# Which PSUM banks take the transposes of layer A's outputs and the samples' product, and at which priority v and the outputs are read

## The chip, the cores and the metric

The kernel runs on one core of a Trainium2 chip. The metric is the device time of one execution in microseconds. A core has five engines that run side by side and meet at semaphores: TensorE (PE, matmuls and transposes), VectorE (DVE), ScalarE (ACT), GpSimd (POOL) and SyncE (SP, which issues the transfers). PE writes its results to PSUM, eight banks, from where ACT and DVE read them. A bank can be given to the next tile only when everything that reads the tile before has ended.

## What is computed

A decoder trunk of two layers for a prompt of 1024 tokens and 8 samples of one token each, side by side as 1032 columns, in float32. Layer A is HGRN2, a gated linear recurrence; layer B is a gated MLP over chunks of 128 tokens. Each is followed by a gated input embedding. The change touches layer A alone. Its core, cut from the reference:

```python
proj = h @ w_in
q, f, i, z = jnp.split(proj, [D_MODEL, 2 * D_MODEL, 2 * D_MODEL + D_INNER], axis=-1)
q = jax.nn.silu(q)                     # 8 heads of 128
logf = jnp.logaddexp(jnp.log(lb), jnp.log1p(-lb) + jax.nn.log_sigmoid(f))
k = -jnp.expm1(logf)
v = i                                  # 8 heads of 256
# S_t = diag(f_t) S_(t-1) + k_t v_t^T,  o_t = S_t^T q_t
o, S = hgrn2_chunkwise(q, k, v, logf, s0)
o = rmsnorm(o, g_norm)                 # over the 256 values of a head
return (o * jax.nn.silu(z)) @ w_out, S
```

The prompt starts from a state of zero; each sample brings its own state, which is updated by one token and multiplied with its q.

## The kernel before

**Precision.** Matmuls work on fp32 numbers that are split in two parts: `split` (L224) has ACT write the rounded high part (L225, named with h: `vh`, `kh`, `Sh`) and DVE the remainder (L226, named with l). `mm3` (L228) makes one product of three matmuls, L230 to L232. Both halves of a split read the same source, so a PSUM bank that is split is held until DVE's L226 has run.

**Tiling.** The 1032 columns come in three chunks of 384, 384 and 264. For each of the eight heads `head_proj` (L695) runs the projections for f, q and v, each into a tile `ps_proj` of the tag mm. Of q, ACT makes a sigmoid (`sg`, L616) and DVE multiplies (L617). Of v, ACT copies to `vf` (L717), PE transposes in blocks of 128 to `pt_v` (L760) and `split` makes `vh` and `vl`, with the samples' eight rows copied to `vs` (L763). `decay` (L801) makes the products of the forget gates (L813 to L822 and L848, most of DVE's work) and, through `visit`, the within-chunk attention in two further banks (`pC`, `pD`). `recur` (L892) goes through the blocks of 128 rows: `pd`, the state's update, and `po`, the output. `out_sum` (L872) has ACT copy the output to `on` (L876) and sum its squares (L877); `out_scale` (L880) adds epsilon on DVE (`ss_e`, L883) and takes the power on POOL (`rsq`, L239); ACT scales `on` (L935); `out_transpose` (L886) turns it by PE to `pt_o` (L889), and DVE multiplies `pt_o` with the gate to `oz` (L942). `sample` (L952) does the same for the eight samples: the product with the states is `pos` (L984), and its `pt_o` is read by DVE at L997.

**The PSUM banks.** In layer A the eight banks are: three of tag mm, in turn for `ps_proj`, `pt_k` (the transposes of k, L862), `pt_o` of the sample, and, at the end, `ps_pple` of the next stage; one of tag po for `po` and `pos`; one of tag pt for `pt_v` and the `pt_o` of the prompt; two for `pC` and `pD`; one for `pd`. From the time at which the last head's projections begin (`last_head`), `pos` is in mm; that holds for the samples of head 6 and of head 7.

**What sets the order.** PE's order is that of the program: generators that are spawned on a clock (`Ticks`, L49) and resumed after so many ticks (`yield`). One tick passes with each projection. The orders of the other engines are made by a scheduler that estimates times and goes by priority; `tc.high_priority(offset=PRI)` with `PRI = 400` puts what it encloses ahead of 400 later instructions' worth of program. ACT, DVE and SP therefore change their order if the priority or the bank of one instruction changes, and every engine runs its own order strictly.

Of the kernel before, what the change touches and what calls it, by code (L numbers as in the profile page):

```python
# [8 lines left out]
F32 = mybir.dt.float32  # L9
# [8 lines left out]
P = 128  # L18
# [8 lines left out]
DV = 256  # L27
# [3 lines left out]
PRI = 400  # L31
# [13 lines left out]
NT = (3, 3, 2)  # L45
# [37 lines left out]
def trunk_kernel(ctx, tc, xT, st, pT, nrm, wina, lbl, gna, wouta, winb, lng, lnb, lngr, lnbr,  # L83
# [7 lines left out]
    def pool(stack, name, bufs=1, **kw):  # L91
        return stack.enter_context(tc.tile_pool(name=name, bufs=bufs, reuse_waits="tile", **kw))
# [5 lines left out]
    pp = pool(ctx, "psum", space=PSUM)  # L98
# [125 lines left out]
    def split(hi, lo, src, eng=V):  # L224
        last["split"] = A.copy(hi, src)  # L225
        last["lo"] = eng.tensor_tensor(lo, src, hi.bitcast(F32), ALU.subtract)  # L226
# [393 lines left out]
    def new_head():  # L620
        return dict(f=[], qk=[], vh=[], vl=[], zs={}, dec={}, oz={})
# [73 lines left out]
    def head_proj(h, r):  # L695
# [9 lines left out]
        else:  # L705
            for c in CH:
                tk.spawn(decay(h, r, c), 1 + 5 * c)
        r["vs"] = wa.tile([NS, DV], F32, name="vs", bufs=1)
        tk.spawn(sample(h, r), 1)
        tk.spawn(recur(h, r), 1)  # L710
        for m in range(2):
# [42 lines left out]
    def v_token_major(h, r, m, c, vf):  # L754
        if not m:
            r["vh"].append(wa.tile([P, NT[c], DV], F32R, name=f"vh{c}"))
            r["vl"].append(wa.tile([P, NT[c], DV], F32R, name=f"vl{c}"))
        pt = pp.tile([P, 3, P], F32, name="pt_v", tag="pt", bufs=1)
        for i in range(NT[c]):
            PE.transpose(pt[:, i, :], vf[:, i * P:(i + 1) * P], ident)  # L760
        if c == 2:
            PE.transpose(pt[:NS, 2, :], vf[:, 256:264], ident)
            V.tensor_copy(r["vs"][:, m * P:(m + 1) * P], pt[:NS, 2, :])  # L763
        split(r["vh"][c][:, :, m * P:(m + 1) * P], r["vl"][c][:, :, m * P:(m + 1) * P], pt[:, :NT[c], :])
        if m:
            r[f"v{c}"] = True
        return
        yield
# [101 lines left out]
    last_head = [False]  # L870

    def out_sum(po, ss):  # L872

        on = wa.tile([P, DV], F32, name="on", bufs=6)
        with tc.high_priority(offset=PRI if last_head[0] else 0):
            A.copy(on, po)  # L876
            A.activation(po, po, AF.Square, accum_out=ss)  # L877
        return on

    def out_scale(ss, n):  # L880
        e = wa.tile([P, n], F32, name=f"ss_e{n}", bufs=2)
        with tc.high_priority(offset=PRI):
            V.tensor_scalar(e, ss, DV * EPS, None, ALU.add)  # L883
        return rsqrt(wa, e, n)

    def out_transpose(on, tag="pt", bufs=1):  # L886
        pt = pp.tile([P, 2, P], F32, name="pt_o", tag=tag, bufs=bufs)
        for m in range(2):
            PE.transpose(pt[:, m, :], on[:, m * P:(m + 1) * P], ident)  # L889
        return pt  # L890

    def recur(h, r):  # L892

        S = Sh = Sl = None
        for c in CH:
            yield lambda: c in r["dec"] and r.get(f"v{c}")
            ah, al, qh, ql, kh, kl, t128 = r["dec"][c]
            ss = wa.tile([P, 3], F32, name="ss", bufs=2)
            ons = []
            for i in range(NT[c]):  # L900
                n = OFF[c] // P + i
                vh, vl = r["vh"][c][:, i, :], r["vl"][c][:, i, :]
                pd = pa.tile([P, DV], F32, name="pd", bufs=1)
                po = pp.tile([P, DV], F32, name="po", tag="po", bufs=1)
                mm3(pd, blk(kh, i), blk(kl, i), vh, vl, True, True)
                mm3(po, blk(ah, i), blk(al, i), vh, vl, True, n == 0)
                if n:
                    mm3(po, blk(qh, i), blk(ql, i), Sh, Sl, False, True)
                Sn = wa.tile([P, DV], F32, name="S", bufs=2)
                with tc.high_priority(offset=PRI):  # L910
                    if n == 0:
                        V.tensor_copy(Sn, pd)
                    else:
                        V.scalar_tensor_tensor(Sn, S, t128[:, i:i + 1], pd, ALU.mult, ALU.add)
                    S = Sn
                    if n < 7:
                        Sh = wa.tile([P, DV], F32R, name="Sh", bufs=2)
                        Sl = wa.tile([P, DV], F32R, name="Sl", bufs=2)
                        split(Sh, Sl, S)
                if n == 7:  # L920
                    nc.sync.dma_start(so_p[h], S)
                ons.append(out_sum(po, ss[:, i:i + 1]))
                yield 2
            tk.spawn(finish(h, r, c, ss, ons), 1)

    def finish(h, r, c, ss, ons):

        n = NT[c]
        if h < NH - 1:
            r["zs"][c] = wa.tile([P, 2, W[c]], F32, name=f"zs{c}")  # L930
            nc.sync.dma_start(r["zs"][c], zd[h][c])
            r[f"z{c}"] = True
        y = out_scale(ss[:, :n], n)
        for i in range(n):
            A.activation(ons[i], ons[i], AF.Copy, scale=y[:, i:i + 1])  # L935
        yield OD[0]
        yield lambda: r.get(f"z{c}")
        oz = r["oz"][c] = wa.tile([P, 2, 384], F32, name="oz", bufs=2)
        for i in range(n):
            pt = out_transpose(ons[i])  # L940
            with tc.high_priority(offset=PRI):
                V.tensor_tensor(oz[:, :, i * P:(i + 1) * P], pt, r["zs"][c][:, :, i * P:(i + 1) * P], ALU.mult)  # L942
            yield 1
        if c < 2:
            spill(h, r, c)
            spilled.add((h, c))

    def spill(h, r, c):
        w = W[c]
        nc.sync.dma_start(ozd[c][:, 2 * h:2 * h + 2, :], r["oz"][c][:, :, :w])  # L950

    def sample(h, r):  # L952

        q, f, k = r["qk"][2][:, 0, :], r["f"][2], r["qk"][2][:, 1, :]
        qs = wa.tile([P, 3, NS], F32, name="qs", bufs=1)
        G.tensor_copy(qs[:, 0, :], f[:, 256:264])
        G.tensor_copy(qs[:, 1, :], k[:, 256:264])
        qmv = qm.rearrange("p (c two) x -> p c (two x)", two=2)
        G.tensor_copy(qmv[:, :, 0:34:33], q[:, 256:264].rearrange("p (c two) -> p c two", two=2))
        Ss = []  # L960
        for j in range(2):
            S0 = wa.tile([P, 4, DV], F32, name="S0", bufs=2)

            nc.sync.dma_start(S0, st[h].rearrange("p (c two) v -> p two c v", two=2)[:, j])
            Ss.append(S0)
        yield lambda: r.get("v2")
        vd = dram.tile([NS, DV], F32, name=f"vd{h}")
        nc.sync.dma_start(vd, r["vs"])
        for j in range(2):
            S0 = Ss[j]  # L970
            vb = wa.tile([P, 4, DV], F32, name="vb", bufs=1)
            nc.sync.dma_start(vb, vd.rearrange("(c two) v -> two c v", two=2)[j].partition_broadcast(P))
            yield 2
            for c in range(4):
                b = 2 * c + j
                A.activation(S0[:, c, :], S0[:, c, :], AF.Copy, scale=qs[:, 0, b:b + 1])
                V.scalar_tensor_tensor(S0[:, c, :], vb[:, c, :], qs[:, 1, b:b + 1], S0[:, c, :],  # L977
                                       ALU.mult, ALU.add)
            nc.sync.dma_start(so_s[h].rearrange("p (c two) v -> p two c v", two=2)[:, j], S0)
        yield 4  # L980
        pos = pp.tile([P, DV], F32, name="pos", tag="mm" if last_head[0] else "po", bufs=3 if last_head[0] else 1)
        for j in range(2):
            for c in range(4):
                PE.matmul(pos[32 * c:32 * c + 32, :], qm[:, 2 * c + j, :], Ss[j][:, c, :],  # L984
                          start=j == 0, stop=j == 1)
        ss = wa.tile([P, 1], F32, name="ss1", bufs=1)
        on = out_sum(pos, ss)
        yield 1
        y = out_scale(ss, 1)
        A.activation(on, on, AF.Copy, scale=y)  # L990
        yield OD[1]
        yield lambda: r.get("z2") and 2 in r["oz"]
        pt = out_transpose(on, "mm", 3)
        oz = r["oz"][2]
        pv = pt.rearrange("p m (c x) -> p m c x", x=32)[:, :, :, 0:2]
        for m in range(2):
            V.tensor_tensor(oz[:, m, 256:264].rearrange("p (c x) -> p c x", x=2), pv[:, m],  # L997
                            r["zs"][2][:, m, 256:264].rearrange("p (c x) -> p c x", x=2), ALU.mult)
        yield 5
        spill(h, r, 2)  # L1000
# [12 lines left out]
    for h in range(NH):  # L1013
# [5 lines left out]
        r = new_head() if h else r0  # L1019
# [705 lines left out]
```

## Time and profile before

| | us |
|---|---|
| median of three runs | 1908.05 |
| lowest and highest | 1906.54, 1909.65 |
| the profiled execution | 1910.62 |
| its span in the trace | 1908.8 |

The page lists for each engine the time in which it was busy; PE's weight loads (PEld) run beside its matmuls. A row of the table of waits reads: engine, tile and line that waited, what it waited for last, microseconds in total, times, longest. A row of the windows gives a stretch of time, its length, the busy time of PE, PEld, DVE, ACT and POOL with the number of instructions, then the clock that was granted to PE (1.00 is full speed), the busy share of the transfer engines and GB/s. A row of the timeline gives start, duration, engine, line, operation, output and inputs, and in brackets the idle time of the engine ahead of it and what ended that.

The span in 40 slices, busy tenths of PE and of the clock:

PE 8999989899899898999999999999999999999997, clock 9 tenths or more throughout. One slice is 47.7 us; the second to the eighth head of layer A fill about the sixth to the sixteenth.

### The profile page before, as it was taken

What the parts mean: (1) busy time and instruction counts of PE and PEld (TensorE: products, weight loads), DVE (VectorE), ACT (ScalarE), POOL (GpSimd) and SP (SyncE); (2) the same over time, 40 slices, a digit from 0 to 9 for tenths busy, and PEclk for the clock granted to TensorE, in tenths of its full rate; (3) what the DMA queues carried; (4) which work ended last, traced back from release to release, by engine and by line L of the source; (5) the groups of instructions that cost most, each with busy time, mean ns of one, the idle gap of its engine ahead of it and who ended that gap; (6) DMA issues with size and microseconds to landing.
All of it is one profiled execution on the core that took longest, in us unless ns stands there. A gap on an engine that the chain in (4) does not pass through costs nothing.

```text
span 1908.8 us, 37135 instructions
## 1 busy us (share of the span) xinstructions
PE 1834.5 (96%) x14458; PEld 1795.6 (94%) x14458; DVE 1367.6 (72%) x2760; ACT 898.2 (47%) x1905; POOL 410.9 (22%) x407
## 2 busy tenths in 40 slices
PE   8999989899899898999999999999999999999997
PEld 7999988898889898999999999999999999999997
DVE  7765878678788677678583955567778878777655
ACT  6533455565465554625353644443333345434442
POOL 4000011111111110000042433344444542000222
PEclk9999999999999999999999999999999999999999
DMA  6233333335443335765233343323334546954223
GB/s 215 78 110 106 116 113 114 103 119 163 135 135 115 103 122 175 249 231 183 82 102 133 117 144 99 101 77 110 110 113 137 177 146 198 300 180 126 71 89 112
DMA packets 164560, 258.11 MB, mean 135 GB/s; under 512 B 16096, under 2 KB 136864, under 8 KB 163360
## 3 DMA queue, kind: packets, MB, share of 16 engines
q1 hardware_dynamic: 164384, 255.74, 42.3%
q8 instruction: 113, 1.85, 0.4%
q14 instruction: 63, 0.52, 0.1%
HBM read 182.88 MB, written 72.80 MB: 134 GB/s over the span
## 4 chain that ended last, share of the span: by engine, by line
PE 63%; DVE 18%; DMA 9%; ACT 4%; issue 3%; POOL 2%; SPq 1%; DVEq 0%; POOLq 0%; ACTq 0%
PE ps_proj L230 15%; PE ps_proj L231 15%; PE ps_proj L232 15%; PE ps_d L230 2%; PE ps_d L232 2%; PE ps_d L231 2%; DMA vb<-vd 2%; PE ps_o L230 2%; PE ps_o L232 2%; PE ps_o L231 2%; DVE wlo L152 1%; DVE S L977 1%; POOL rsq L239 1%; DVE qk L848 1%; DVE M L818 1%
## 5 line engine op out<-in xcount | busy, mean ns | idle before, releaser
L230 PE MATMUL ps_proj<-bh,whi 128*128 128x264 f32 (+1 forms) x2248 | 721.1, 321 | 1.4 <-ACT u L493 1.4
L231 PE MATMUL ps_proj<-bl,whi 128*128 128x264 f32 (+1 forms) x2248 | 705.1, 314 | 4.9 <-DVE bl L226 2.4
L232 PE MATMUL ps_proj<-bh,wlo 128*128 128x264 f32 (+1 forms) x2248 | 704.2, 313 | 1.0 <-DVE wlo L152 1.0
L231 PEld LDWEIGHTS ps_proj<-bl,whi 128*128 128x128 f32 x2248 | 427.4, 190 | 8.2 <-DVE bl L226 4.6
L230 PEld LDWEIGHTS ps_proj<-bh,whi 128*128 128x128 f32 x2248 | 427.1, 190 | 3.8 <-ACT u L493 1.9
L232 PEld LDWEIGHTS ps_proj<-bh,wlo 128*128 128x128 f32 x2248 | 426.1, 190 | 1.9 <-DVE wlo L152 1.9
L152 DVE TENSOR_TENSOR wlo<-wstg,whi 128x1024 fp32r<-128x1024 f32 x148 | 185.5, 1254 | 111.3 <-ACT whi L151 110.9
L151 ACT CAST whi<-wstg 128x1024 fp32r<-128x1024 f32 x148 | 155.2, 1049 | 141.8 <-PE ps_proj L231 120.9
L151 ACT CAST shi<-ssum 128x512 fp32r<-128x512 f32 x152 | 94.1, 622 | 189.6 <-PE ps_proj L231 88.7
L152 DVE TENSOR_TENSOR slo<-ssum,shi 128x512 fp32r<-128x512 f32 x152 | 114.2, 754 | 9.3 <-ACT shi L151 8.9
L239 POOL TENSOR_TENSOR rsq<-rms_e,mhalf 128x3 f32<-128x3 f32 x15 | 17.8, 1187 | 365.1 <-DVE rms_e L284 361.4
L230 PE MATMUL ps_proj<-xmh,shi 128*128 128x384 f32 x244 | 82.8, 340 | 0.3 <-DVE u L497 0.3
L232 PE MATMUL ps_proj<-xmh,slo 128*128 128x384 f32 x244 | 81.7, 335 | 0.0
L231 PE MATMUL ps_proj<-xml,shi 128*128 128x384 f32 x244 | 81.6, 335 | 0.0
L848 DVE TENSOR_TENSOR qk<-qk,t 128x384 f32<-128x384 f32 (+1 forms) x144 | 74.4, 520 | 7.9 <-PE pC L798 7.3
L230 PE MATMUL ps_o<-bh,whi 128*128 128x384 f32 (+1 forms) x232 | 73.2, 316 | 0.0
L232 PE MATMUL ps_o<-bh,wlo 128*128 128x384 f32 (+1 forms) x232 | 72.7, 313 | 0.0
L231 PE MATMUL ps_o<-bl,whi 128*128 128x384 f32 (+1 forms) x232 | 72.7, 313 | 0.0
L1516 POOL TENSOR_TENSOR s<-s,u 128x384 f32<-128x384 f32 (+1 forms) x48 | 54.6, 1138 | 69.4 <-DVE s L1510 68.8
L239 POOL TENSOR_TENSOR rsq<-ss_e,mhalf 128x3 f32<-128x3 f32 (+2 forms) x32 | 29.2, 912 | 172.5 <-DVE ss_e L883 160.4
L1255 DVE TENSOR_TENSOR tmp<-tmp,pj 128x384 f32<-128x384 f32 (+1 forms) x48 | 25.6, 533 | 55.9 <-ACT tmp L1254 52.2
L266 POOL TENSOR_TENSOR ssq<-ssq,tmp 128x384 f32<-128x384 f32 (+1 forms) x36 | 34.3, 953 | 108.0 <-ACT tmp L265 108.0
(376 smaller groups left out, 4146.5 us busy)
## 6 DMA issues: line engine op xcount, KB each, us to landing
wstg<-in_wina SPq DMA_DIRECT2D x48, 512.0 KB, 3.7
wstg<-in_winb SPq DMA_DIRECT2D x48, 512.0 KB, 4.0
pj<-ppd SPq DMA_DIRECT2D x16, 516.0 KB, 5.0
S<-in_st SPq DMA_DIRECT2D x16, 512.0 KB, 4.5
vb<-vd SPq DMA_DIRECT2D x16, 512.0 KB, 4.6
out_so_s<-S SPq DMA_DIRECT2D x16, 512.0 KB, 3.5
wstg<-in_wouta SPq DMA_DIRECT2D x16, 512.0 KB, 5.5
wstg<-in_wgate SPq DMA_DIRECT2D x16, 512.0 KB, 3.7
```

Of the source, the lines that this page charges most:

```text
L151: A.copy(hi, src)
L152: V.tensor_tensor(lo, src, hi.bitcast(F32), ALU.subtract)
L230: PE.matmul(ps, wh, xh, start=first, stop=False, skip_group_check=more)
L231: PE.matmul(ps, wh, xl, start=False, stop=False, skip_group_check=more)
L232: PE.matmul(ps, wl, xh, start=False, stop=last, skip_group_check=more)
L239: G.tensor_tensor(y, e, mhalf[:, :n], ALU.pow)
L266: eng.tensor_tensor(ssq, ssq, sq[:, :w], ALU.add)
L818: V.reciprocal(yv[:, :, 4:8], xv[:, :, 4:8])
L848: V.tensor_tensor(lev, lev, t2.rearrange("p two (n o) -> p two n o", o=1).broadcast_to([P, 2, n, lv]), ALU.mult)
L977: V.scalar_tensor_tensor(S0[:, c, :], vb[:, c, :], qs[:, 1, b:b + 1], S0[:, c, :], ALU.mult, ALU.add)
L1255: V.tensor_tensor(gt[:, :w], gt[:, :w], pj[:, OFF[c]:OFF[c] + w], ALU.mult)
L1516: G.tensor_tensor(s[:, :w], s[:, :w], us[mm, c][:, :w], ALU.mult)
```

## The change

1. `v_token_major`: the split of `pt_v` into `vh` and `vl` gets high priority.
2. `out_sum`: ACT's copy and square of an output always have high priority, not only in the last head.
3. `out_transpose`: every `pt_o` is in tag mm, three banks, not only the sample's; tag pt is left to `pt_v`.
4. `sample`: `pos` is always in tag mm; tag po is left to `po`.

```diff
--- before.py
+++ after.py
@@ -761,7 +761,8 @@
         if c == 2:
             PE.transpose(pt[:NS, 2, :], vf[:, 256:264], ident)
             V.tensor_copy(r["vs"][:, m * P:(m + 1) * P], pt[:NS, 2, :])
-        split(r["vh"][c][:, :, m * P:(m + 1) * P], r["vl"][c][:, :, m * P:(m + 1) * P], pt[:, :NT[c], :])
+        with tc.high_priority(offset=PRI):
+            split(r["vh"][c][:, :, m * P:(m + 1) * P], r["vl"][c][:, :, m * P:(m + 1) * P], pt[:, :NT[c], :])
         if m:
             r[f"v{c}"] = True
         return
@@ -872,7 +873,7 @@
     def out_sum(po, ss):
 
         on = wa.tile([P, DV], F32, name="on", bufs=6)
-        with tc.high_priority(offset=PRI if last_head[0] else 0):
+        with tc.high_priority(offset=PRI):
             A.copy(on, po)
             A.activation(po, po, AF.Square, accum_out=ss)
         return on
@@ -883,8 +884,8 @@
             V.tensor_scalar(e, ss, DV * EPS, None, ALU.add)
         return rsqrt(wa, e, n)
 
-    def out_transpose(on, tag="pt", bufs=1):
-        pt = pp.tile([P, 2, P], F32, name="pt_o", tag=tag, bufs=bufs)
+    def out_transpose(on):
+        pt = pp.tile([P, 2, P], F32, name="pt_o", tag="mm", bufs=3)
         for m in range(2):
             PE.transpose(pt[:, m, :], on[:, m * P:(m + 1) * P], ident)
         return pt
@@ -978,7 +979,7 @@
                                        ALU.mult, ALU.add)
             nc.sync.dma_start(so_s[h].rearrange("p (c two) v -> p two c v", two=2)[:, j], S0)
         yield 4
-        pos = pp.tile([P, DV], F32, name="pos", tag="mm" if last_head[0] else "po", bufs=3 if last_head[0] else 1)
+        pos = pp.tile([P, DV], F32, name="pos", tag="mm", bufs=3)
         for j in range(2):
             for c in range(4):
                 PE.matmul(pos[32 * c:32 * c + 32, :], qm[:, 2 * c + j, :], Ss[j][:, c, :],
@@ -990,7 +991,7 @@
         A.activation(on, on, AF.Copy, scale=y)
         yield OD[1]
         yield lambda: r.get("z2") and 2 in r["oz"]
-        pt = out_transpose(on, "mm", 3)
+        pt = out_transpose(on)
         oz = r["oz"][2]
         pv = pt.rearrange("p m (c x) -> p m c x", x=32)[:, :, :, 0:2]
         for m in range(2):
```

Lines behind L763 are one higher after the change. The instructions are the same on every engine; PE's and POOL's orders are the same row by row. What moves is ACT's, DVE's and SP's order, and which bank a tile is in.

**DVE, third head, where v's last block is split.** Names: `M` and `qk` with L813 to L823 and L848/L849 are the decays of the third chunk; `pC` and `al` the attention; `vl<-pt_v` the split; `oz<-pt_o` the outputs, and that of 8 columns (L997/L998) the sample's. Before:

```order
L226 TENSOR_TENSOR al<-pC,ah 128x384
L818 RECIPROCAL M<-M 128x32x4
L226 TENSOR_TENSOR vl_4541<-pt_v,vh_4540 128x2x128
L819 TENSOR_TENSOR M<-qk,M 128x256
L820 TENSOR_TENSOR M<-qk,M 128x256
L942 TENSOR_TENSOR oz<-pt_o,zs_4388 128x2x128
L848 TENSOR_TENSOR qk<-qk,t_4527 128x2x24x8
L822 TENSOR_TENSOR qk<-qk,f 128x256
L848 TENSOR_TENSOR qk<-qk,f 128x2x128
L848 TENSOR_TENSOR qk<-qk,t_4568 128x2x12x16
L848 TENSOR_TENSOR qk<-qk,t_4650 128x2x64x2
L997 TENSOR_TENSOR oz<-pt_o,zs_4388 128x8 x2
```

After:

```order
L818 RECIPROCAL M<-M 128x32x4
L226 TENSOR_TENSOR vl_4541<-pt_v,vh_4540 128x2x128
L943 TENSOR_TENSOR oz<-pt_o,zs_4388 128x2x128
L226 TENSOR_TENSOR al<-pC,ah 128x384
L819 RECIPROCAL M<-M 128x32x4
L849 TENSOR_TENSOR qk<-qk,t_4527 128x2x24x8
L820 TENSOR_TENSOR M<-qk,M 128x256
L821 TENSOR_TENSOR M<-qk,M 128x256
L849 TENSOR_TENSOR qk<-qk,t_4568 128x2x12x16
L998 TENSOR_TENSOR oz<-pt_o,zs_4388 128x8 x2
L226 TENSOR_TENSOR kl<-pt_k,kh 128x384
L943 TENSOR_TENSOR oz<-pt_o,zs_4388 128x2x128
```

The split and the first `oz` now stand ahead of the second reciprocal, the sample's read ahead of three qk products, and the third `oz` and `kl` come directly behind it.

**PE and DVE, second head, around the samples' product.** On PE, the same before and after but for the line numbers: the last projection matmul of q's second chunk, `pos`, one `pt_o`, and the first projection matmul of the third chunk.

```order
L232 MATMUL ps_proj<-bh_137,wlo 128x384
L984 MATMUL pos<-S_3251,qm 32x256 x4
L984 MATMUL pos<-S_3253,qm 32x256 x4
L889 MATMUL pt_o<-ident,on 128x128 x2
L230 MATMUL ps_proj<-bh_138,whi 128x264
```

In banks: before, `pos` is in po and `pt_o` in pt, and `ps_proj` takes the next mm bank. After, `pos` and `pt_o` take the next two mm banks, and `ps_proj` the third, which holds the projection of q that ended just ahead of `pos` until DVE has read it at L617. On DVE at that place, before:

```order
L883 TENSOR_SCALAR ss_e_4244<-ss 128x3
L848 TENSOR_TENSOR qk<-qk,f 128x2x192
L851 TENSOR_TENSOR t_4513<-t_4359 128x3
L848 TENSOR_TENSOR qk<-qk,t_4291 128x2x96x2
L848 TENSOR_TENSOR qk<-qk,t_4316 128x2x48x4
L617 TENSOR_TENSOR qk<-ps_proj,sg 128x384
L942 TENSOR_TENSOR oz<-pt_o,zs_4034 128x2x128
L819 TENSOR_TENSOR M<-qk,M 128x384
```

After:

```order
L884 TENSOR_SCALAR ss_e_4244<-ss 128x3
L849 TENSOR_TENSOR qk<-qk,f 128x2x192
L852 TENSOR_TENSOR t_4513<-t_4359 128x3
L849 TENSOR_TENSOR qk<-qk,t_4291 128x2x96x2
L849 TENSOR_TENSOR qk<-qk,t_4316 128x2x48x4
L617 TENSOR_TENSOR qk<-ps_proj,sg 128x384
L943 TENSOR_TENSOR oz<-pt_o,zs_4034 128x2x128
L820 TENSOR_TENSOR M<-qk,M 128x384
```

L617 keeps its neighbours: `ss_e`, three qk products, then L617, then `oz`.

**DVE, last head, where the loads for the next stage begin.** `bl_139<-zstg` is the split of gated outputs that were spilled and are loaded again, `wlo<-wstg` that of weights, `zs` the gate. Before:

```order
L383 TENSOR_TENSOR bl_139<-zstg,bh_136 128x768 x2
L647 SCALAR_TENSOR_TENSOR zs_9939<-ps_proj,gn_813,sg 128x384
L914 SCALAR_TENSOR_TENSOR S<-S,t_9736,pd 128x256
L226 TENSOR_TENSOR Sl<-S,Sh 128x256
L883 TENSOR_SCALAR ss_e_10264<-ss 128x3
L383 TENSOR_TENSOR bl_139<-zstg,bh_136 128x768 x2
L942 TENSOR_TENSOR oz<-pt_o,zs_9939 128x2x128
L152 TENSOR_TENSOR wlo<-wstg,whi 128x1024
```

After:

```order
L383 TENSOR_TENSOR bl_139<-zstg,bh_136 128x768 x2
L647 SCALAR_TENSOR_TENSOR zs_9939<-ps_proj,gn_813,sg 128x384
L915 SCALAR_TENSOR_TENSOR S<-S,t_9736,pd 128x256
L226 TENSOR_TENSOR Sl<-S,Sh 128x256
L884 TENSOR_SCALAR ss_e_10264<-ss 128x3
L383 TENSOR_TENSOR bl_139<-zstg,bh_136 128x768
L152 TENSOR_TENSOR wlo<-wstg,whi 128x1024
L943 TENSOR_TENSOR oz<-pt_o,zs_9939 128x2x128
```

`wlo` has passed the second `bl` and the `oz`. That `oz` reads the `pt_o` behind `pos`, and the `ps_proj` that follows on PE now takes that `pt_o`'s bank.

## The prediction

> **What bounds the kernel now.** I began with the page's busy times.
>
> ```profile
> span 1908.8 us, 37135 instructions
> PE 1834.5 (96%) x14458; PEld 1795.6 (94%) x14458; DVE 1367.6 (72%) x2760; ACT 898.2 (47%) x1905; POOL 410.9 (22%) x407
> ```
>
> TensorE (PE) is busy for 1834.5 of 1908.8 us, so only time in which PE stands still, or runs at a lower clock, can be won. Next come the windows: they say where PE stands still.
>
> ```profile
> 262.00:790.00 528.00, 482.00 (x4840) 460.73 (x4839) 397.60 (x977) 293.43 (x769) 65.60 (x89) 0.97 0.41 130
> 100.00:262.00 162.00, 160.09 (x1286) 158.05 (x1285) 117.85 (x239) 68.16 (x144) 6.99 (x16) 1.00 0.38 115
> ```
>
> The second to the eighth head of layer A and the last one's tail lie between 262 and 790 us: PE busy for 482.0 of 528 us (91%), mean granted clock 0.97. In the stretch ahead of them it is 99% and 1.00. So 46 of the 74 idle microseconds lie where the change acts, and VectorE (DVE) is busy for only 75% of that stretch: PE waits there for the order of DVE's work more than for its amount. The table of PE's waits names the places.
>
> ```profile
> PE pt_o L889 <- DVE vl L226: 20.8, 7, 4.7
> PE pt_v L760 <- DVE oz L942: 11.6, 15, 3.7
> PE po L230 <- ACT pos L877: 6.4, 5, 1.5
> PE pos L984 <- ACT po L877: 3.3, 3, 1.2
> ...
> PE pt_o L889 <- DVE oz L942: 2.9, 5, 1.2
> ...
> PE po L230 <- ACT po L877: 1.1, 1, 1.1
> ```
>
> These rows sum to 46.1 us, and all come from two PSUM banks: pt_o and pt_v share that of tag pt, pos and po that of tag po. The change aims at every one. Last comes the clock around one of the seven pt_o stalls.
>
> ```profile
> 361.40:364.80 3.40, 1.41 (x9) 1.09 (x7) 3.40 (x8) 1.14 (x3) 0.36 (x1) 1.00 0.39 155
> 364.80:368.20 3.40, 2.79 (x10) 2.82 (x11) 3.19 (x10) 0.51 (x1) 0.00 (x0) 0.50 0.02 5
> 272.63:279.46 6.83, 4.16 (x14) 4.16 (x15) 2.93 (x13) 2.73 (x8) 0.19 (x1) 0.50 0.00 0
> ```
>
> The column behind POOL is the granted clock. PE idles 1.99 us of the first stretch; the next 3.4 us run at 0.50. In the second head 6.83 us run at half. So a stall costs its length and then some matmuls at half speed, and a wait that goes gives both back.
>
> Here a rule of the Trainium skill can be weighed. "TensorE: Matmul & The Clock Gate", section "What's actually happening", has the clock halved after at least one idle window of about 3.4 us. This trace disagrees: 1.99 us idle in a stretch of 3.40 us was enough. By the rule stalls of 2 us would cost no clock; I go by the trace.
>
> **The change part by part.** PE's order is the same row by row, and nothing is added to or taken from any engine's work; only banks and the order on ACT, DVE and SP change. So every term is a wait of PE that goes or comes.
>
> *The pt_o stall (seven times).* The place in the third head, in time order, DVE and PE:
>
> ```profile
> 362.79 0.93 DVE L817 RECIPROCAL M<-M 128x128 f32<-128x128 f32 x1
> ...
> 363.65 0.48 DVE L226 TENSOR_TENSOR al<-pC,ah 128x384 fp32r<-128x384 f32 x1
> ...
> 364.06 0.93 DVE L818 RECIPROCAL M<-M 128x128 f32<-128x128 f32 x1
> ...
> 364.92 0.35 DVE L226 TENSOR_TENSOR vl<-pt_v,vh 128x256 fp32r<-128x256 f32 x1
> ...
> 365.41 0.66 PE L889 MATMUL pt_o<-ident,on 128*128 128x128 f32 x2 [2.60 <-DVE vl L226]
> ...
> 365.52 0.41 DVE L820 TENSOR_TENSOR M<-qk,M 128x256 f32<-128x256 f32 x1
> ...
> 366.11 0.42 DVE L942 TENSOR_TENSOR oz<-pt_o,zs 128x256 f32<-128x256 f32 x1 [0.18 <-PE pt_o L889]
> ...
> 366.45 0.55 DVE L848 TENSOR_TENSOR qk<-qk,t 128x384 f32<-128x384 f32 x1
> ...
> 366.51 0.52 PE L232 MATMUL ps_proj<-bh,wlo 128*128 128x384 f32 x1
> ...
> 366.83 0.52 PE L230 MATMUL ps_proj<-bh,whi 128*128 128x384 f32 x1
> ...
> 368.50 0.34 PE L230 MATMUL ps_proj<-bh,whi 128*128 128x384 f32 x1
> ...
> 368.68 0.34 PE L231 MATMUL ps_proj<-bl,whi 128*128 128x384 f32 x1
> ...
> 369.03 0.38 PE L889 MATMUL pt_o<-ident,on 128*128 128x128 f32 x2
> ...
> 369.45 0.24 DVE L997 TENSOR_TENSOR oz<-pt_o,zs 128x8 f32<-128x8 f32 x2 [0.85 <-PE pt_o L889]
> ...
> 369.58 0.38 PE L889 MATMUL pt_o<-ident,on 128*128 128x128 f32 x2
> ```
>
> PE is ready at 365.41 - 2.60 = 362.81. pt_o needs the bank that vl still reads, and vl stands behind two reciprocals. With its own bank pt_o runs at 362.8. The twelve matmuls behind it are then at full speed: starts 0.18 apart (368.50 to 368.68), not 0.32 (366.51 to 366.83), so 2.1 us from 363.1 to 365.2. Then come the sample's pt_o and pt_k, 0.55 as between 369.03 and 369.58, and PE stands at the next pt_o at 365.75. There is the **new wait**: three banks now carry ps_proj, pt_k and all pt_o, and this pt_o takes the bank of the sample's pt_o, which DVE must read first (oz at L997). In the new order that read stands behind vl, oz, al, a reciprocal, a qk product, the two products of L819 and L820, and another qk product. From 363.72, the end of L817, that is 0.35 + 0.42 + 0.48 + 0.93 + 0.55 + 0.41 + 0.41 + 0.55 + 0.24 = 4.3 us by the durations, some 0.4 less since starts lie closer than ends: about 367.8. PE waits some 2.05 us instead of 2.60, and goes on at 367.8 where it did at 369.58. Gain 1.8 us; in five heads 9 us. It lies between nothing, if DVE is no earlier, and 3.8 (369.58 - 365.75), if the read is on time.
>
> The two others differ. In the second head no sample's transposition stands between the two pt_o; I take 3.5 of its stall and half-clock matmuls as gained. In the eighth the wait was the longest:
>
> ```profile
> 723.13 0.62 PE L889 MATMUL pt_o<-ident,on 128*128 128x128 f32 x2 [4.71 <-DVE vl L226]
> ```
>
> Here vl comes late on DVE either way, and the read at L997 stays behind it: 2.5 us, between 0 and 4.7. Together: 15 us.
>
> *The pt_v wait.* pt_v then shares its bank with nothing but pt_v, and 11.6 us go. Of these, 3.7 stand in the second head at the half-clock stretch quoted above, with the 1.1 of po behind po (ACT's reads of po go earlier); about twelve matmuls at 0.32 rather than 0.18 make 1.6 more. Less a new wait of about 1 us for a bank that two DVE instructions of 0.55 hold, this is 5.4 us. The fourteen others hold 7.9 us and are followed by nothing that waits. Together 13.3, between 8 and 16.
>
> *The samples' product.* pos leaves the bank of po, so the 6.4 and 3.3 us go. But it, and the pt_o right behind it, take two of the three mm banks, and the next ps_proj needs the third, which holds the projection of q that ended just ahead of pos; DVE must have read that at L617. From the same timeline in the third head, and in the seventh head, where pos is in mm already:
>
> ```profile
> 404.92 0.37 ACT L877 ACTIVATE po<-po 128x256 f32<-128x256 f32 x1
> ...
> 406.65 0.37 PE L230 MATMUL ps_proj<-bh,whi 128*128 128x264 f32 x1
> ...
> 407.94 0.47 ACT L616 ACTIVATE sg<-ps_proj 128x384 f32<-128x384 f32 x1
> ...
> 408.19 0.28 PE L230 MATMUL pd<-vh,kh 128*128 128x256 f32 x1
> ...
> 408.44 0.56 DVE L617 TENSOR_TENSOR qk<-ps_proj,sg 128x384 f32<-128x384 f32 x1 [0.87 <-ACT sg L616]
> ...
> 410.17 0.39 PE L230 MATMUL po<-vh,ah 128*128 128x256 f32 x1 [1.47 <-ACT pos L877]
> ...
> 692.17 0.37 PE L230 MATMUL ps_proj<-bh,whi 128*128 128x264 f32 x1
> ...
> 693.49 0.56 DVE L617 TENSOR_TENSOR qk<-ps_proj,sg 128x384 f32<-128x384 f32 x1 [0.86 <-ACT sg L616]
> ```
>
> ps_proj now starts at 406.65 and would have to wait until 409.00, the end of L617: 2.35 us. Behind it on PE are 1.54 us of ps_proj (406.65 to 408.19) and about 0.4 of pd, then po: 410.9 rather than 410.17. So where 1.47 us of waiting goes, 0.75 us is lost in sum. Five heads: -3.75. In the seventh no old wait is there to give back: 692.17 to 694.05 is 1.9 us lost. Sum -5.7, between 0 (ACT's sigmoid of L616 keeps ahead of PE) and -14 (six times 2.35).
>
> *The priorities alone.* ACT's square of po, 0.37 us in the row at 404.92, now stands ahead of the cast of the state Sh that the next po needs. Twelve matmuls of ps_proj, 1.5 us or more, lie between, and hide it: nothing. Without that cover it would be 0.4 us in each of the chunks of 128 rows. The split of v ahead of DVE's other work is already in the 4.3 us above.
>
> *The last head.* pt_o follows pos in mm, and the ps_proj behind pt_o takes pt_o's own bank, so it waits for oz, which stands behind wlo on DVE:
>
> ```profile
> 763.45 0.42 PE L230 MATMUL ps_proj<-bh,whi 128*128 128x384 f32 x1
> ...
> 764.87 1.92 DVE L383 TENSOR_TENSOR bl<-zstg,bh 128x768 fp32r<-128x768 f32 x2 [1.31 <-ACT bh L379]
> ...
> 767.04 1.22 DVE L152 TENSOR_TENSOR wlo<-wstg,whi 128x1024 fp32r<-128x1024 f32 x1
> ```
>
> wlo ended at 768.26. In the new order one of the two L383 ahead of it stands behind it, so I put its end 1 us earlier (1.92 / 2), near 767.3, and oz at 767.7: 4.3 us of waiting at 763.45. Of the old waits of pt_o for oz about 1.5 go here, and the ps_pple behind share the rotation, another 1.5 lost. Term -4.3, between +1.5 and -8. Behind PE's wait at this place all of the last head's recurrence queues up.
>
> **Sum at full clock:** 15 + 13.3 - 5.7 - 4.3 = 18.3 us. **The clock:** the new waits of 2.05 us (six) and 2.35 us (six) are as long as what halved it at 361.4, but a wait that falls across two stretches need not. The old waits of 1.5 us and less have no half clock behind them. I count seven in ten, each at ten matmuls times 0.14 (0.32 - 0.18) = 1.4 us: twelve times 0.7 times 1.4 is 11.8, and 1.4 for the last head: -13. Net gain 5 us. The profiled execution took 1910.6 us, 1.8 more than its span, and 2.6 more than the median of 1908.05; taking the gain from the median I predict 1903.
>
> **The rivals.**
> - *The clock holds:* the new waits do not halve it. Gain 18, 1890. For it: they follow a denser row of matmuls; against it the 1.99 us above. Chance 0.12. The section of the Trainium skill named above would give the same.
> - *Every targeted wait goes and nothing takes its place:* 46.1 us and eight half-clock stretches of 1.5, about 1850. Against it are the three new waits above. Chance 0.05 for anything under 1880.
> - *The bank rotation is the bound:* slower. pos and pt_o leave one mm bank to ps_proj, so once in each of six heads PE waits for L617, whose sigmoid stands on ACT behind the scalings of the outputs. If each comes 1 us later than I took (-6), the last head loses its 8 and every one of the thirteen new waits halves the clock (-18 instead of -13), the sum is 18 - 6 - 4 - 18 = -10: 1917. It decides from a wait of about 3 us at ps_proj in each head: there the 18 us are used up. Against it: L617 follows PE's own progress. The page "TensorE: Matmul & The Clock Gate" of the Trainium skill, section "A second HAM failure mode: psum-queue depth-cycling", speaks for it: short idling between groups as PSUM banks are cycled lets the clock swing. The half clocks of this trace follow stalls of that very kind. Chance 0.18.
> - *No change:* the terms cancel to within 3.8 us. Chance 0.25. My sum lies at its edge.
>
> **How the numbers follow.** The forecast, a gain between 4 and 13 us, has 0.40. Faster by over 0.2% (about what a measurement of this kernel can tell from no change): 0.40 + 0.12 + 0.05 = 0.57; within it 0.25; slower 0.18. The range runs from 1886 (the clock holds, and a little more at pt_o) to 1915 (nearly the slower rival): less than a tenth is left out on each side.
>
> **What would show it.** Right: pt_o behind vl and pt_v behind oz are gone from PE's waits; ps_proj behind qk of L617 is there six times at 2 to 3 us, pt_o behind oz of L998 (formerly L997) six times at about 2, ps_proj behind oz once at about 4; the clock between 262 and 790 us stays near 0.97. Wrong: ps_proj never waits for L617 (then 1893), or the clock there is 1.00, or DVE runs the read at L998 ahead of the reciprocal.

## The result, and the profile after

| | us |
|---|---|
| before, median of four runs | 1908.85 (1906.54 to 1910.18) |
| changed, median of four runs | 1891.38 (1887.13 to 1896.58) |
| ratio, with its 95% interval | 0.9911 (0.9882 to 0.9940) |
| profiled execution of the change, and its span | 1893.27, 1891.2 |

The change makes the kernel 17.5 us faster. The forecast was a gain of 5 us, and 4 to 13 us were called likeliest; the range given holds the result, and 1890 was the figure of the rival "the clock holds". The page's first lines, the windows, and the table of PE's waits, of the changed kernel:

```profile
span 1891.2 us, 37108 instructions
...
PE 1830.6 (97%) x14458; PEld 1795.8 (95%) x14458; DVE 1364.7 (72%) x2760; ACT 896.3 (47%) x1905; POOL 408.3 (22%) x407
```

```profile
262.00:790.00 528.00, 495.67 (x4955) 478.98 (x4954) 409.36 (x996) 299.27 (x781) 62.78 (x89) 0.97 0.44 141
```

```profile
PE ps_proj L230 <- DVE qk L617: 12.5, 6, 3.5
PE pt_o L890 <- DVE oz L998: 11.3, 6, 2.3
PE ps_proj L230 <- DVE oz L943: 5.7, 2, 4.2
...
PE pd L230 <- DVE S L915: 1.8, 1, 1.8
...
PE pt_k L863 <- DVE qk L617: 0.8, 1, 0.8
```

In the stretch of 528 us PE is busy for 495.7 instead of 482.0 us (more of the program falls into it, 4955 matmuls instead of 4840), and the mean clock is 0.97 as before. The six rows shown of before, 46.1 us, are gone but for 0.3. In their place stand three waits that the kernel before did not have: six for L617, six for L998, one of 4.2 us for oz in the last head. About 32 us of waiting remain where 46 were.

Since PE's order is the same in both kernels, each matmul can be compared with itself. Starts from the two timelines, and by how much the changed kernel is ahead:

| matmul | before | after | ahead by |
|---|---|---|---|
| second head, pt_k | 258.47 | 258.45 | 0.0 |
| second head, pt_v behind its stalls | 311.08 | 300.32 | 10.8 |
| second head, po behind pos | 339.53 | 330.65 | 8.9 |
| third head, second transposition of pt_v behind pt_o | 370.64 | 358.22 | 12.4 |
| third head, po behind pos | 410.17 | 398.03 | 12.1 |
| seventh head, second transposition of pt_v behind pt_o | 656.20 | 633.76 | 22.4 |
| seventh head, fifth matmul of po behind pos | 694.53 | 675.53 | 19.0 |
| eighth head, the third pt_o | 727.58 | 702.74 | 24.8 |
| tail, pt_o among ps_pple | 781.14 | 762.90 | 18.2 |
| the end of the span | | | 17.6 |

So the third to the seventh head win some 4 us each where v is transposed, and the second to the seventh give back between 0.3 and 4.1 at the samples' product (not all of these places are in the table); the tail gives back 6.6.

The stall at pt_o, in the third head, by the timeline of the changed kernel:

```profile
353.03 0.38 PE L890 MATMUL pt_o<-ident,on 128*128 128x128 f32 x2
353.15 0.93 DVE L818 RECIPROCAL M<-M 128x128 f32<-128x128 f32 x1
...
354.01 0.35 DVE L226 TENSOR_TENSOR vl<-pt_v,vh 128x256 fp32r<-128x256 f32 x1
354.29 0.40 DVE L943 TENSOR_TENSOR oz<-pt_o,zs 128x256 f32<-128x256 f32 x1
...
355.09 0.93 DVE L819 RECIPROCAL M<-M 128x128 f32<-128x128 f32 x1
...
357.49 0.23 DVE L998 TENSOR_TENSOR oz<-pt_o,zs 128x8 f32<-128x8 f32 x2
...
357.86 0.41 PE L890 MATMUL pt_o<-ident,on 128*128 128x128 f32 x2 [1.80 <-DVE oz L998]
```

pt_o runs ahead of vl now. The sample's read ends 3.64 us behind the end of the first reciprocal (354.08 to 357.72), and the next pt_o waits 1.80 us for it.

### The profile page after: what moved, and what is told of

It is laid out like the page before. It is cut to its first block, busy times and chain, and to the rows that moved or that the text cites. A ratio compares the mean times of both kernels' runs of the same rounds, so it can differ in the third digit from the quotient of the medians.

```text
span 1891.2 us, 37108 instructions
## 1 busy us (share of the span) xinstructions
PE 1830.6 (97%) x14458; PEld 1795.8 (95%) x14458; DVE 1364.7 (72%) x2760; ACT 896.3 (47%) x1905; POOL 408.3 (22%) x407
## 4 chain that ended last, share of the span: by engine, by line
PE 73%; DVE 14%; DMA 6%; ACT 3%; issue 2%; POOL 2%; SPq 0%; DVEq 0%; ACTq 0%; POOLq 0%
PE ps_proj L230 17%; PE ps_proj L231 17%; PE ps_proj L232 17%; PE ps_d L230 3%; PE ps_d L232 3%; PE ps_d L231 3%; PE ps_o L230 2%; PE ps_o L232 2%; PE ps_o L231 2%; DMA vb<-vd 2%; PE psp L1508 1%; DVE S L978 1%; DVE wlo L152 1%; DVE M L819 1%; DVE qk L849 1%
## 5 line engine op out<-in xcount | busy, mean ns | idle before, releaser
L230 PE MATMUL ps_proj<-bh,whi 128*128 128x264 f32 (+1 forms) x2248 | 719.9, 320 | 20.1 <-DVE qk L617 12.5
L152 DVE TENSOR_TENSOR slo<-ssum,shi 128x512 fp32r<-128x512 f32 x152 | 113.1, 746 | 11.3 <-ACT shi L151 10.8
L849 DVE TENSOR_TENSOR qk<-qk,t 128x384 f32<-128x384 f32 (+1 forms) x144 | 74.7, 520 | 9.9 <-PE pC L799 7.6
```

What stands on the lines that cost most here:

```text
L152: V.tensor_tensor(lo, src, hi.bitcast(F32), ALU.subtract)
L230: PE.matmul(ps, wh, xh, start=first, stop=False, skip_group_check=more)
L849: V.tensor_tensor(lev, lev, t2.rearrange("p two (n o) -> p two n o", o=1).broadcast_to([P, 2, n, lv]), ALU.mult)
```

## The experiments

Each run leaves PE's work as it is; what differs is banks and priorities. "Half-clock stretches" below are counted in one profile of each, between 255 and 800 us, in windows of 0.4 us whose granted clock is under 0.95; before has 8, the change 7. The kernel before ran beside each group: 1908.83 us with the first four, 1909.90 with the next, 1906.14 with the last.

| run | median us | ratio to before (95%) | half-clock stretches |
|---|---|---|---|
| pos in po (e1) | 1877.41 | 0.9833 (0.9811 to 0.9855) | 1 |
| sample's pt_o in po (e2) | 1883.48 | 0.9869 (0.9843 to 0.9896) | 5 |
| two priorities only (e3) | 1891.92 | 0.9912 (0.9890 to 0.9934) | 2 |
| banks only (e4) | 1893.11 | 0.9920 (0.9899 to 0.9940) | 7 |
| e1 and e2 together (e5) | 1868.86 | 0.9783 (0.9758 to 0.9807) | 1 |
| e5 with pos in pt (e6) | 1870.14 | 0.9788 (0.9764 to 0.9812) | 1 |
| before, pos in mm only (e7) | 1910.59 | 1.0004 (0.9993 to 1.0016) | 7 |
| the change again (e8) | 1899.36 | one execution | 6 |
| before, split's priority only (e9) | 1893.28 | 0.9929 (0.9914 to 0.9944) | 2 |
| before, reads' priority only (e10) | 1908.05 | 1.0009 (0.9996 to 1.0021) | 9 |
| before, pt_o in mm only (e11) | 1876.82 | 0.9842 (0.9827 to 0.9857) | 2 |
| e5 without priorities (e12) | 1870.61 | 0.9807 (0.9785 to 0.9829) | 1 |

**Are the new waits the banks? pos in po (e1).**

```diff
-        pos = pp.tile([P, DV], F32, name="pos", tag="mm", bufs=3)
+        pos = pp.tile([P, DV], F32, name="pos", tag="po", bufs=1)
```

> The change, but with the samples' product pos always in the bank of po (also in the last head). Theory (the waits of ps_proj for L617 come from pos and the pt_o behind it taking two of three mm banks, and the 4.2 us wait for oz in the last head from pos, pt_o and ps_proj sharing the rotation): ps_proj behind qk of L617 (12.5 us, 6 times) and ps_proj behind oz at the last head (4.2) disappear; po behind ACT's square of pos and pos behind that of po come back with 7 to 10 us, since these five places had 9.7 before. pt_o behind oz of L998 stays at 11 us. Some 7 to 10 us less than the change: 1881 to 1885. Rival (L617 is late for PE whatever the banks, the pair only names it): ps_proj or pt_o still wait for L617 or its neighbours, and the time stays within 3 us of the change's 1891.

```profile
PE pt_o L890 <- DVE oz L998: 11.4, 6, 2.3
PE po L230 <- ACT pos L878: 6.8, 7, 1.3
...
PE ps_proj L230 <- DVE oz L943: 2.0, 2, 1.6
...
PE pos L985 <- ACT po L878: 1.3, 1, 1.3
```

These are PE's waits in that run. L617 is gone from them, the last head's 4.2 us too; po and pos wait 8.1 us again. The theory holds for the mechanism. The time fell by 14 instead of 7 to 10; the half-clock stretches went from 7 to 1, which the expectation had not counted and which is the likeliest source of the rest, though no run separates the two.

**The sample's pt_o in po (e2).** `out_transpose` gets its tag back as an argument for it:

```diff
-        pt = out_transpose(on)
+        pt = out_transpose(on, "po", 1)
```

> The change, but the sample's pt_o goes into the bank of po, not into mm. Theory (the wait at L998 is for the bank of the sample's pt_o, which the next pt_o takes): pt_o behind oz of L998 (11.3 us, 6 times) disappears, the waits for L617 (12.5) stay; 9 to 11 us less than the change: 1880 to 1882. Rival (DVE is simply late there, and PE meets the same order one instruction later): the wait reappears at pt_v, ps_proj or po in the same six places with 8 us or more, and the time is within 3 us of 1891.

```profile
PE ps_proj L230 <- DVE qk L617: 13.6, 6, 3.7
PE ps_proj L230 <- DVE oz L943: 5.3, 2, 3.9
...
PE pt_v L760 <- DVE vl L226: 1.9, 1, 1.9
```

The wait for L998 is gone in all six heads; only the eighth has another in its place, 1.9 us at pt_v. The time fell by 8, slightly less than expected.

**Priorities only, banks only (e3, e4).** The parts of the diff were left out crosswise: e3 has the two `high_priority` lines on the kernel before, e4 the two tiles' tags.

> The kernel before with the two priorities alone (split of v, reads of the outputs); all banks as before. Theory (both parts shorten the pt_o stall, by different means): DVE's vl stands directly behind the first reciprocal, about 1.3 us earlier, so pt_o behind vl falls from 20.8 to 9 to 12 us, and with stalls of 1.3 us most of the half-clock stretches behind them go; pt_v behind oz stays at 11 us, po and pos as before. 1893 to 1899. Rival (the banks alone make the gain, the priorities only move ACT's reads): within 3 us of 1908.

```profile
PE pt_o L890 <- DVE vl L226: 13.1, 7, 4.7
PE pt_v L760 <- DVE oz L943: 12.3, 15, 4.2
```

> The change without the two priorities: only pt_o and pos move to mm. Theory: pt_o behind vl and pt_v behind oz are gone, but the read of the sample's pt_o stays behind the second reciprocal and vl, so that pt_o behind oz of L997 is as long as or longer than 1.8 us (11 to 16 us in six), with some half-clock stretches back; ps_proj behind L617 as in the change (12 to 14). 1892 to 1898. Rival (the priorities make the gain): 1903 or more.

```profile
PE ps_proj L230 <- DVE qk L617: 12.3, 6, 2.5
PE pt_o L889 <- DVE oz L997: 9.1, 6, 2.3
```

Each half of the change gains as much as the whole: 0.9912 and 0.9920 beside 0.9911. They do not add up. In e3 pt_o still waits for vl, but 13.1 us instead of 20.8, and the half-clock stretches fall from 8 to 2: five stalls shrink from 2.60 to 1.33 us, and none of those halves the clock. In e4 that stall is gone at once, so vl's place on DVE counts for little (one wait of 0.4 us at pt_v), and the new waits appear instead. Its wait at L997 is shorter than expected (9.1, not 11 to 16): in its order on DVE one qk product less stands ahead of the sample's read.

**Which priority, which bank (e9, e10, e11, e7).** Each is the kernel before with one edit:

```diff
 e9
+        with tc.high_priority(offset=PRI):
             split(r["vh"]...
 e10
-        with tc.high_priority(offset=PRI if last_head[0] else 0):
+        with tc.high_priority(offset=PRI):
 e11
-    def out_transpose(on, tag="pt", bufs=1):
+    def out_transpose(on, tag="mm", bufs=3):
 e7
-        pos = pp.tile([P, DV], F32, name="pos", tag="mm" if last_head[0] else "po", bufs=3 if last_head[0] else 1)
+        pos = pp.tile([P, DV], F32, name="pos", tag="mm", bufs=3)
```

> The kernel before with only the split of v at high priority. Theory (the gain of the two priorities is vl ahead of the second reciprocal: the pt_o stall falls from 2.60 to 1.3 us and no longer halves the clock): pt_o behind vl 13 us, po behind pos 6 to 7 as before, half-clock stretches left only in the second and the eighth head; 1894 to 1898. Rival (the earlier reads of po on ACT do it): pt_o behind vl stays near 20 and the time at 1905 to 1909.

> The kernel before with only ACT's copy and square of the outputs at high priority. Theory: po behind pos and pos behind po fall from 9.7 to about 5 us, pt_o behind vl stays at 20 with its half-clock stretches; 1903 to 1907. Rival (these reads are the part that counts): 1898 or less, with pt_o behind vl below 15.

> The kernel before with only every pt_o in mm; pos as before, no priority. Theory (the gain of the banks is pt_o's, and pos in mm costs more than it gives): pt_o behind vl and pt_v behind oz gone, pt_o behind oz of L997 9 us, ps_proj behind L617 only in the seventh head (2 us), po behind pos 7 to 10, the last head's wait for oz at 4; half-clock stretches fewer than the change's: 1884 to 1889, below banks only (1893). Rival (pos in mm is needed for the gain): 1895 or more.

> The kernel before with only pos always in mm; pt_o stays in pt, no priority changed. Theory (it takes pos and pt_o together to leave ps_proj one bank): no wait for L617; po behind pos and pos behind po (9.7 us) are gone; pt_o behind vl with its half-clock stretches as before; 1898 to 1901. Rival (pos in mm is enough to make ps_proj wait): ps_proj behind qk of L617 with 8 us or more in five or six places, and 1905 to 1912.

PE's waits of e11, and behind them those of e7:

```profile
PE pt_o L889 <- DVE oz L997: 9.0, 6, 2.3
PE po L230 <- ACT pos L877: 6.1, 5, 1.5
PE ps_proj L230 <- DVE oz L942: 5.1, 2, 4.0
...
PE ps_proj L230 <- DVE qk L617: 1.7, 1, 1.7
```

```profile
PE pt_o L889 <- DVE vl L226: 20.6, 7, 4.7
PE pt_v L760 <- DVE oz L942: 11.6, 15, 3.7
PE pt_o L889 <- DVE oz L942: 8.4, 11, 1.1
PE pt_v L760 <- ACT vf L717: 3.3, 6, 2.0
```

The split's priority alone makes the gain of e3 (0.9929), the reads' priority none (1.0009, and pt_o behind vl stays at 20.6). In e9 the theory holds. In e10 its waits came as expected, po behind pos and pos behind po 5.4 us together instead of 9.7, but no time was won: 1908.05 is above the range of 1903 to 1907, and the profile has one half-clock stretch more than that of before. pt_o in mm alone gains 1.6%, more than the whole change, and more than was expected of it. Its one wait for L617 is in the seventh head, where pos is in mm already; that is the pair's doing once more. Adding pos in mm for all heads (e4) takes half of it back: 0.9920.

e7 came out as neither the theory nor the rival had it. The time is the rival's, but its cause is not there: no ps_proj waits for L617 (one pt_k does, 1.0 us). The 9.7 us of po and pos are gone, yet no time is won: pt_o behind oz rises from 2.9 to 8.4 us and pt_v behind vf from 1.0 to 3.3 (1.2 of that in the first head, at 213 us), which is 7.8 back. With po's bank out of the way, the single bank of pt is what PE meets next, some microseconds later.

**A version beyond both (e5, e6, e12).** e5 joins e1 and e2; e6 has pos in pt instead of po; e12 is e5 without the two priorities.

> The change with both edits of the first two runs: pos and the sample's pt_o in the bank of po, the prompt's pt_o in mm. Theory (the two waits are two banks, independent of each other): ps_proj behind L617 and pt_o behind L998 both near 0, po behind pos stays at 7 us, no half-clock stretch from them; 1877 less 11: 1865 to 1868. Rival (with one wait gone PE meets the other earlier): at least 6 us of new waits between the two places and 1871 or more.

> As the run before, but pos goes into the bank of pt_v, whose next user comes some 14 us later. Theory (po behind pos, 6.8 us in seven places, and pos behind po, 1.3, are the bank alone): both disappear and nothing takes their place: 8 us less than with both in po, 1857 to 1860. Rival (po then waits for the state's cast Sh on ACT or another step of the recurrence, which the wait for pos only hid): the waits move to po behind Sh, Sl or ah, and the time falls by less than 3 us.

> The fastest so far (pos and the sample's pt_o in the bank of po, the prompt's pt_o in mm) without the two priorities. Theory (priorities and banks shorten the same stall by two means, so that with these banks the priorities have nothing left to win there): po behind pos and pos behind po about 2 us more than with them (7.9), nothing else; 1869 to 1873. Rival (the two add up): pt_o, pt_v or po wait 8 us or more in addition, and the time is 1880 or more.

The waits of e5, of e6 and of e12:

```profile
PE po L230 <- ACT pos L878: 7.1, 7, 2.7
PE ps_d L230 <- DVE c L516: 5.3, 4, 2.7
```

```profile
PE ps_proj L230 <- DVE oz L943: 5.2, 7, 1.6
...
PE pt_v L760 <- ACT vf L717: 3.3, 6, 1.2
```

```profile
PE po L230 <- ACT pos L877: 6.1, 6, 1.4
PE pos L984 <- ACT po L877: 5.2, 4, 1.9
```

e5 is 2.2% faster than before and 1.3 points better than the change; the two waits are two banks, and both go. Its 1868.86 us is 0.9 above the range expected. e6 shows a limit: po behind pos is gone, but ps_proj behind oz and pt_v behind vf take about its place, and no time is won. So its theory failed, and the rival had the time right but not the place: po behind Sl is only 1.1 us. e12 cannot be told from e5 (the intervals overlap), though po and pos wait 11.3 us in it instead of 7.9: with these banks, the priorities are worth nothing that these runs show.

**Where the clock is halved (e8).** The changed kernel, unedited, once more:

> The changed kernel itself, once more, for a second profile. Theory (whether a wait of 1.7 to 2.3 us halves the clock depends on where it falls against stretches of 3.4 us that run on their own): the waits are the same in size within 0.2 us, but half-clock stretches stand at other places than in the first profile (there behind four of the six waits for L617 and one of the six for L998), and the time differs by several us with their number. Rival (the length or the kind of wait decides): the same places show half clock as in the first profile.

Most of the waits agree within 0.2 us (11.7 us for L617 in all, 11.3 for L998). Three do not: the longest for L617 is 2.7 us instead of 3.5, the last head's is 4.8 instead of 4.2, and pd's 1.8 us at 737 us is gone. Four half-clock places are the same as in the first profile, and in the last head the half clock starts 3.4 us earlier and lasts twice as long; that at 737, behind the wait of pd, is missing. Of the waits for L617 the one at 327 halves the clock in the first profile and that at 396 in the second, and each lasts 1.67 or 1.68 us in both. So for these two neither length nor place in the program decides, as the theory has it; at the four that agree the rival's outcome stands. The windows of the first profile, in pairs: a step in which PE waits, laid out so that it ends where the half clock starts, and the step behind it:

```profile
324.02:327.43 3.41, 1.74 (x21) 0.71 (x19) 2.51 (x8) 2.02 (x6) 1.08 (x1) 1.00 0.26 67
327.43:330.84 3.41, 3.41 (x16) 3.41 (x17) 2.00 (x6) 2.28 (x8) 0.60 (x1) 0.51 0.72 246
392.28:395.69 3.41, 2.17 (x23) 1.10 (x21) 2.51 (x8) 1.50 (x4) 1.08 (x1) 1.00 0.07 24
395.69:399.10 3.41, 2.98 (x25) 2.99 (x26) 3.25 (x9) 2.76 (x10) 0.60 (x1) 1.00 0.85 290
354.73:358.14 3.41, 1.61 (x13) 1.37 (x12) 3.41 (x9) 1.40 (x3) 0.00 (x0) 1.00 0.00 0
358.14:361.55 3.41, 3.41 (x26) 3.41 (x25) 3.05 (x8) 0.96 (x2) 0.00 (x0) 1.00 0.51 159
699.48:702.89 3.41, 1.09 (x10) 0.85 (x9) 3.41 (x10) 0.85 (x2) 0.00 (x0) 1.00 0.00 0
702.89:706.30 3.41, 3.41 (x14) 3.41 (x14) 3.24 (x9) 0.48 (x1) 0.00 (x0) 0.51 0.40 138
```

All eight lie on one grid of 3.413 us (324.02 to 702.89 is 111 steps), and so does the start of every half clock from the second to the eighth head: 327.5, 464.1, 535.7, 672.3 and 703.0 us are 40, 21, 40 and 9 steps apart. The Trainium skill, "TensorE: Matmul & The Clock Gate", section "What's actually happening", has a window of 3413 ns that runs on its own; the grid agrees with that. The wait at 327 lies wholly within one step (PE busy 1.74 us of it), the one at 396 across two (2.17 in the first): the first halves the clock, the second does not. The waits for L998 leave PE busy for 1.61 us of a step and do not halve it, that of 2.3 us in the eighth head, with 1.09, does.

e8 took 1899.36 us beside 1893.27 for the first profile. The half clock in layer A does not explain these 6 us: matmul by matmul the second profile is 0.7 us ahead at 1581 us and 5.5 behind at 1674, far behind layer A, in a part that the change does not touch. Its table of waits has the place:

```profile
PE ps_d L230 <- DVE c L516: 4.2, 3, 3.2
...
1668.96:1672.37 3.41, 1.14 (x7) 0.82 (x5) 3.41 (x7) 0.00 (x0) 0.00 (x0) 1.00 0.65 223
1672.37:1675.78 3.41, 2.52 (x8) 2.52 (x9) 3.41 (x7) 0.62 (x1) 0.00 (x0) 0.50 0.74 229
1675.78:1679.20 3.42, 3.42 (x15) 3.42 (x14) 1.15 (x3) 0.00 (x0) 0.00 (x0) 0.50 0.30 110
```

The first profile has 0.2 us in that row, and full clock at this place. So between these two executions one wait of 3.2 us and the half clock behind it (6.8 us) make the difference; why `c` was late there in one of them stays open.

## Why the prediction was right, and where it was off

**What bounds it: right.** PE's waits in layer A set the end; 46.1 us of them were the stake, and all of them went but 0.3.

**The new waits: right in place and number, and near in size.** Predicted six waits for L617 of 2.35 us (1.9 in the seventh head), six for L998 of 2.05 and one for oz of 4.3; measured 12.5 us in six (1.67 to 3.50 each), 11.3 in six (1.80 in five, 2.32 in the eighth head) and 4.2. e1 and e2 show that each is a bank: give the tile another one, and the wait is gone.

**The samples' product: right in sum.** Predicted -5.7 at full clock and -5.9 for the clock, -11.6; by the starts in the two timelines the six places together cost 11.4, unevenly: 0.3 in the third head, 4.1 in the fourth. That this part of the change is a loss, as the step said, is shown by e11 against e4 and e1 against the change. That pos alone gains nothing on the kernel before (e7) was not foreseen: the step took it that the old waits of po would simply go.

**The second head: near.** 10.0 predicted (5.4, 3.5 and two pt_v of 0.56), 10.8 measured.

**The pt_o stall and pt_v in the third to seventh head: the step that was mis-sized.** Predicted 1.8 + 0.5 + 0.6 = 2.9 us a head at full clock, less 1.0 for the clock (seven in ten times 1.4); measured between 3.5 and 4.3 a head, 19.6 in the five against 9.5. Half of the difference is the clock: the step took the new wait, 2.05 us, to be as long as what halves it; it came out at 1.80, and in none of the five heads was the clock halved. The other half is the size at full clock. pt_o with the pt_v behind it brought 2.8 us in the third head and 3.1 in the four others, where 2.3 was summed: the read at L998 came 0.25 us earlier, and the sum was made from the third head alone. The pt_v ahead of it brought 0.7 to 1.2 where 0.6 was taken.

**The eighth head:** 2.5 was taken at pt_o, with bounds of 0 and 4.7, 1.1 for two pt_v, and 1.0 less for the clock: 2.6. It brought 5.8, of which 4.0 at pt_o and 1.8 ahead of it; that pt_o's new wait of 2.3 us did halve the clock.

**The last head and the tail:** predicted -4.3 and -1.4 for the clock, measured -6.6. A wait of 1.8 us at pd (for the state at L915), with half clock behind it, was not foreseen; it is not there in the second profile (e8).

**The priorities:** the step priced the reads of po at nothing, and e10 shows nothing. It counted the split's priority within the pt_o term. What it missed is that this one line on the kernel before would have won as much as the whole change (e9): the two are two cures of one stall, of which the second finds nothing left.

**The rivals.** "The clock holds" gave 1890, next to the measured 1891, but that is luck: the clock fell behind four of the six waits for L617, one of the six for L998 and twice in the last head. It held behind the five waits of 1.80 us and two of those for L617, and the larger gain at pt_o made up for the rest. "The bank rotation is the bound" named the right wait with too high a price; its sum of -10 from 1908 is also 1918, not 1917. If ps_proj never waited for L617, the time by the prediction's own terms (1903 less 11.6) would be 1891, not the 1893 given there.

## What to carry to other kernels

Price a bank move by the whole rotation: list, for each tile that moves, whose bank the next tile takes and what must have read it by then. Test the parts of a change singly before you keep them: here one edit (pt_o in mm) gained 1.6%, another took half of that back, a third was a second cure for the same stall, and leaving the harmful one out made the kernel faster than the change. A short wait that no longer halves the clock is worth more than its microseconds, so ask of each stall which side of that it falls on.

## What the runs showed of the hardware

Of two steps of the clock's grid the one in which PE was busier was followed by half clock: 1.74 us at 324.02, while 1.61 us at 354.73 was not. In the first PE spent 1.07 us on the product of the samples, matmuls of 32 columns:

```profile
324.22 1.07 PE L985 MATMUL pos<-S,qm 128*32 128x256 f32 x16
```

That such narrow matmuls count for less where the clock is decided would fit the steps shown so far, but another trace speaks against it. In e2, the first step below holds the same 1.07 us of them and keeps the full clock; the third, far behind layer A, holds none and is followed by half clock:

```profile
725.30:728.71 3.41, 1.72 (x21) 0.65 (x19) 1.56 (x4) 2.71 (x7) 0.85 (x1) 1.00 0.67 216
728.71:732.13 3.42, 1.24 (x7) 1.24 (x8) 3.03 (x6) 3.10 (x8) 0.63 (x1) 1.00 0.46 107
1585.46:1588.87 3.41, 1.68 (x9) 1.04 (x7) 3.41 (x7) 1.57 (x5) 0.72 (x1) 1.00 0.58 171
1588.87:1592.28 3.41, 3.30 (x10) 3.30 (x11) 2.61 (x5) 1.30 (x4) 0.00 (x0) 0.50 0.84 257
```

Each of the fourteen traces can be laid on its own grid in this way. Between 255 and 800 us every step at full clock with less than 1.5 us of busy PE was followed by half clock, and none with more than 1.8 us was. In between both happened: 1.53 us kept the full clock (e5, at 520.69), and 1.75 us did not (e8, at 668.86). What decides there stays open.
